# Merge operands asked for inside the last pair of sequences, and new places for the tiles around it

## The chip, the cores and the metric

The kernel runs on one core of one Trainium2 chip. A core has five engines with a queue of its own each: TensorE (PE, matrix products), VectorE (DVE), ScalarE (ACT), GpSimd (POOL) and SyncE (SP), which here issues most transfers. Each engine takes its instructions in order. The metric is the device time of one execution in microseconds (us).

## What is computed

One layer of a decoder, for a prompt of 1024 tokens and for 8 sample sequences of 4 new tokens each with 2048 old ones in a paged cache. Two mixers (a sparse attention and a short convolution) share one projection; what they give is merged, projected and followed by an MLP. Cut to the parts that the change is about:

```python
def compress(k, pe, w1, w2):            # summaries of overlapping blocks of cached rows
    chunks = ...                        # (sequence, 128 chunks of 16 rows, head, 1024)
    w1r = w1.reshape(2, 16 * 64, 256)
    proj = einsum('bckx,mxh->mbckh', chunks, w1r)
    hid = pe.reshape(-1) @ w1
    for m in range(2):
        hid = hid + proj[m, :, m:m + n_cmp]
    return gelu(hid) @ w2

def merge_and_mlp(x, a, c, ga, gb, w_nsa_out, w_conv_out, w_o, g_mlp, w_up, w_down):
    m = sigmoid(ga) * (a @ w_nsa_out) + sigmoid(gb) * (c @ w_conv_out)
    x = x + m @ w_o
    h = rms_norm(x, g_mlp)
    return x + square(relu(h @ w_up)) @ w_down
```

Every 32-bit operand of a large product is split into a high part (cast to a rounded type, fp32r) and a low part (what is left), and a product is three products: high by high, low by high, high by low.

## The kernel before

Pools of tiles are opened and closed by name on two sides of the on-chip memory, left and right, in the manner of two stacks; a tile with a tag shares `bufs` buffers with the other tiles of that tag, and a new one waits until the old one was last read. The code is written stage after stage, and a scheduler then sets the order on each engine from the dependencies and a timeline of its own; nobody writes the order by hand.

The stages around the change, in the order of the code:

1. Single units. For the first six sequences, `sample_unit` (L639) gathers one sequence's cached keys (`gth`, 1 MB), copies them by heads (`gpr`), transposes them (`ct`), splits them (`cth` on ACT, `ctl` on DVE) and multiplies them by the weight `w1` (`hid`). `blocks_out` (L484) then does the gelu: square on ACT, two operations on POOL (`gt`), tanh on ACT, a last step on DVE (`gx`), and the small products `kvc`, copied into `kcT` (keys) or `vcN` (values). These units run beside the prompt's attention.
2. Pairs. Five times (keys of 6 and 7, then values of 0 to 7) `pair_unit` (L643) does two sequences at once, with one weight product fewer: the sum of the two halves of `w1` (`w2h`, `w2l`) times the odd chunks (n = 0), and each half times a difference of chunks (`dx`, n = 1 and 2). The transposed chunks of a pair are four tiles `xt`, of six buffers; `dx` has one buffer. After n = 0 of a pair the block output of the pair before it is written (`finish()`).
3. Beside the pairs a generator `probs` does the attention of the sample tokens (`sample_group`): window rows, selected rows gathered by POOL (`gk`, four buffers of 0.5 MB), the weights through DRAM (`sl_d`), and in the end the weighted sums `so`, one column block `ownT` per group of four sequences.
4. Merge. `load_aT` (L1301) brings the prompt's attention output back from DRAM in eight tiles `at` and splits it into `aTh`, `aTl`; `load_merge` brings the rows `ta` and `cg` of a column of 128 (528 KB each), `load_wn` the column's weight (`wrd`, 256 KB; high part `whd` on ACT, low part `wld` on POOL through `wsplit`). `merge_in` (L1351) multiplies (`na`, 4 x 3 products for each of the banks 0 to 383, 384 to 767 and 768 to 1055), then DVE and POOL add `ta` and `cg`. The last bank holds the sample columns, for which the new rows of the sample attention (`ts`, from `ownT`) must be there. MJ columns do their first two banks ahead of that.
5. `wo_rows` multiplies the merge by `w_o` in two halves of columns (`wo`, then `c`); in the second half it loads the first half's rows and the input row into `x2` (L1441) and adds (L1455). Then come the norm, the transposes `xT` and the MLP.

What sets the order around the change: SP's queue, where a load waits for the buffer that it writes and everything behind it waits too; POOL's queue, which holds the gathers and the gelu operations; and the scheduler's timeline.

Of the kernel before, what the change touches and what calls it, by code (L numbers as in the profile page):

```python
# [11 lines left out]
F32 = mybir.dt.float32  # L12
F32R = mybir.dt.float32r
# [28 lines left out]
SWB = 2  # L42
MJ = 2
W1B = 9
ATTEND = 5
# [3 lines left out]
UGP = 1  # L49
EB = 3  # L50
ATT = dict(lg=3, pt=2, pv=1, gx=1, gy=1)
PB = 12
WOB = 8
QB = 12
# [65 lines left out]
def tile_hybrid_step(ctx, tc, xp, xs, cck, ccv, csk, csv, swk, swv, sconv, ptab, g_attn, w_in,  # L120
# [33 lines left out]
    def f32(ap):  # L154
        return ap.bitcast(F32)
# [280 lines left out]

    mp = open_pool("cmp", "left")
    pkh = mp.tile([128, HK, 64], F32R, name="pkh")
    pkl = mp.tile([128, HK, 64], F32R, name="pkl")
# [22 lines left out]
    def load_w1(w1, bufs, parts=True, sums=False):  # L462

        out = {}
        for lp in range(8):
            raw = w1p.tile([128, 2, 256], F32, name="w1r", tag="w1r", bufs=2)
            DMA.dma_start(raw, w1[0].rearrange("(m l p) c -> l p m c", m=2, p=128)[lp])
            if parts:
                h, l = (w1p.tile([128, 2, 256], F32R, name="w1" + x, tag="w1" + x, bufs=bufs) for x in "hl")
                S.copy(h, raw)  # L470
                V.tensor_sub(l, raw, f32(h))
                for m in range(2):
                    out[m * 8 + lp] = (h[:, m], l[:, m])
            if sums:
                h, l = (u2.tile([128, 256], F32R, name="w2" + x, tag="w2" + x, bufs=8) for x in "hl")
                V.tensor_add(raw[:, 0], raw[:, 0], raw[:, 1])
                S.copy(h, raw[:, 0])
                V.tensor_sub(l, raw[:, 0], f32(h))
                out[16 + lp] = (h, l)
        return out  # L480
# [147 lines left out]
    def by_heads(raw, q):  # L628
        by_head = up.tile([128, 2, 256], F32, name="gpr", tag="gpr")
# [12 lines left out]
    def pair_unit(kv, cache, b0, w1):  # L642
# [5 lines left out]
        for q in range(4):  # L648
            xt = u2.tile([128, 2, 512], F32, name="xt", tag="xt", bufs=6)
            for s_ in range(2):  # L650
                part = by_heads(raws[s_], q)
                pt = ps(HT["ct"], "ct")
                pv = pt.rearrange("p (i c h) -> p i c h", i=2, h=2)
                for i in range(2):
                    for h in range(2):
                        PE.transpose(pv[:, i, :, h], part[:, h, i * 128:i * 128 + 128], ident)
                S.copy(xt[:, :, s_ * 256:s_ * 256 + 256], pt.rearrange("p (i c) -> p i c", i=2))
            xs.append(xt.rearrange("p i (j e h) -> p i j e h", e=2, h=2))
# [4 lines left out]
        for n in range(3):  # L663
# [3 lines left out]
            for q in range(4):  # L667
                odd = xs[q][:, :, :nj, 1]
                if n:
                    d = up.tile([128, 2, 256], F32, name="dx", tag="gx", bufs=UG)  # L670
                    odd_, d = odd, d.rearrange("p i (j h) -> p i j h", h=2)[:, :, :nj]
                    V.tensor_sub(d, xs[q][:, :, n - 1:n - 1 + nj, 0], odd_)
                    odd = d
# [40 lines left out]

    kc = open_pool("kc", "left")
    kcT = kc.tile([128, NB, 127], F32, name="kcT")
    vcN = kc.tile([127, NB, 128], F32, name="vcN")
    chp = open_pool("cTh", "left")
# [591 lines left out]
    advance(100)  # L1310
    next(behind[0][0])
    close("pa", "cTh")
    u2 = open_pool("u2", "right")
    s1 = open_pool("s1", "left", bufs=2)
    HT.update(ct="ct", hid="hid", sk="sk", sx="sx")
    open_psum(**SMP)
    w1.update(load_w1(w1k, W1B, parts=False, sums=True))
    for i in range(ATTEND + 1, 2 * NB, 2):
# [4 lines left out]
        for n in range(3):  # L1323
            next(unit)
            if n == 0:
                finish()
            for _ in range(SSTEP[i + n % 2] * 2 // 3):
                next(probs, None)
        behind.append((unit, (kv, i % NB + 1)))
    finish()  # L1330
    close("u2", "unit", "gt", "w1")
    ap_ = open_pool("aT", "right")
    aTh = ap_.tile([128, 4, T], F32R, name="aTh")
    aTl = ap_.tile([128, 4, T], F32R, name="aTl")
    ep = open_pool("E", "right")
    wp = open_pool("w", "right", bufs=2)
# [20 lines left out]
    for j in range(MJ):  # L1357
        for i in range(2):
            merge_in(j, *BANKS[i], ("ct", "hid")[i])
    close("s1", "kc")  # L1360
    mpool = open_pool("m", "left")
# [3 lines left out]
    wop = open_pool("wo", "left", bufs=WOB)  # L1365
    for j in range(8):
# [25 lines left out]
    for i, z in enumerate(mT[2]):  # L1392
        P.tensor_copy(m9[:, :, i * 32:i * 32 + 32], f32(z[:, :, 256:]))
    close("w", "E", "aT")

    h2p = open_pool("h2", "right")
# [3 lines left out]
    fp = open_pool("F", "right", bufs=2)  # L1403
    g2 = fp.tile([128, D], F32, name="g2", bufs=1)
# [30 lines left out]
    def wo_rows(half, tt):  # L1435
# [42 lines left out]
    close("wo", "m", "cmp", "att")  # L1478


    wp = open_pool("w", "left", bufs=2)
    qp = open_pool("q", "left")

# [37 lines left out]

    hbp = open_pool("hB", "left")
    t2 = hbp.tile([128, 4, HC], F32, name="t2", tag="t2", bufs=1)
# [84 lines left out]

    rp = open_pool("T", "right")
    dp = open_pool("wd", "right")  # L1610
    wp = open_pool("w", "left")
    up = open_pool("ud", "left")
    lp = open_pool("mlp", "left")
    accp = open_pool("acc", "left")
    accs = [accp.tile([128, 4, HC], F32, name=f"acc{i}") for i in range(4)]
# [82 lines left out]

    op = open_pool("out", "right", bufs=2)
    gf = op.tile([128, D], F32, name="gf", bufs=1)  # L1700
# [126 lines left out]
```

## Time and profile before

| what | us |
|---|---|
| median of 3 timed runs | 1976.39 (1974.79 to 1979.4) |
| the profiled execution, its own time | 1969.69 |
| its span in the trace | 1967.9 |
| PE busy | 1896.1 (96%) |
| DVE, ACT, POOL busy | 1128.0, 860.5, 460.3 |

The pairs lie between about 860 and 1094 us of the span, the merge between 1110 and 1176, the two halves of `w_o` behind it up to about 1276, then the MLP to the end. A row of the trace's timeline gives the start, the duration, the engine, the line, and in brackets how long the engine had been idle and what ended that.

### The profile page before, as it was taken

Reading aid. Unit: us, or ns where it says so; the run is one execution under the profiler, and the core shown is the slowest. Engines: PE = TensorE matmul, PEld = TensorE weight load, DVE = VectorE, ACT = ScalarE, POOL = GpSimd, SP = SyncE. Lnnn points to the kernel's source line nnn. Section 1 sums busy time; section 2 is a strip of 40 time slices with the busy share of each in tenths; the row PEclk is TensorE's granted clock in tenths of the full one; section 3 lists DMA queues with packets and bytes.
Section 4 is the critical chain, followed back from the end, with each engine's and each line's share of the span. In section 5 each row is a group of like instructions: output and inputs, shape, how many; then the busy total and the mean of one; then the engine's idle time right before and its main releaser. Section 6 shows DMA issues by size and latency. Waiting matters only on the chain.

```text
span 1967.9 us, 34867 instructions
## 1 busy us (share of the span) xinstructions
PE 1896.1 (96%) x13172; PEld 1762.2 (90%) x13172; DVE 1128.0 (57%) x2367; ACT 860.5 (44%) x1905; POOL 460.3 (23%) x634
## 2 busy tenths in 40 slices
PE   9999999999999999998999699999999999999998
PEld 7999999999998888876788587789999999999998
DVE  5324232545446766657864552498676655767765
ACT  5113223555456565544542320365455444543443
POOL 3112223433444444433333250130000000000000
PEclk9999999999999999989999799999999999999999
DMA  6365316222236421176544453347756656765664
GB/s 209 126 162 136 97 55 172 65 73 65 69 90 212 148 100 50 47 230 200 180 134 143 163 180 126 122 118 246 245 189 230 225 188 240 258 185 164 182 199 157
DMA packets 238424, 303.77 MB, mean 154 GB/s; under 512 B 20725, under 2 KB 165254, under 8 KB 234160
## 3 DMA queue, kind: packets, MB, share of 16 engines
q1 hardware_dynamic: 231344, 267.99, 43.5%
q0 software_dynamic: 6912, 33.56, 5.0%
q8 instruction: 104, 1.70, 0.4%
q14 instruction: 64, 0.52, 0.1%
HBM read 222.78 MB, written 78.71 MB: 153 GB/s over the span
## 4 chain that ended last, share of the span: by engine, by line
PE 79%; DMA 9%; DVE 4%; issue 3%; ACT 3%; POOL 2%; SPq 1%; POOLq 0%; DVEq 0%; ACTq 0%
PE c L212 9%; PE c L213 9%; PE c L214 9%; PE PT L941 3%; PE ga L213 3%; PE ga L212 3%; PE ga L214 3%; PE hid L213 2%; PE hid L212 2%; DMA wrd<-sd_d 2%; PE hid L214 2%; PE pv L948 2%; PE pv L947 2%; PE so L1233 1%; PE qkv L214 1%
## 5 line engine op out<-in xcount | busy, mean ns | idle before, releaser
L212 PE MATMUL c<-ud,whd 128*128 128x264 f32 x768 | 217.8, 286 | 5.6 <-ACT whd L1623 4.3
L213 PE MATMUL c<-ud,whd 128*128 128x264 f32 x768 | 217.5, 285 | 0.0
L214 PE MATMUL c<-ud,whd 128*128 128x264 f32 x768 | 217.4, 285 | 0.0
L867 POOL TENSOR_SCALAR P<-P,st,gates 128x256 f32<-128x256 f32 (+4 forms) x272 | 151.4, 578 | 125.7 <-DVE st L863 103.7
L212 PEld LDWEIGHTS c<-ud,whd 128*128 128x128 f32 x768 | 144.5, 189 | 6.1 <-ACT whd L1623 4.5
L212 PE MATMUL c<-hBt,wuh 128*128 128x264 f32 x512 | 146.5, 286 | 2.1 <-ACT p L1512 2.1
L214 PE MATMUL c<-hBt,wul 128*128 128x264 f32 x512 | 146.1, 285 | 0.0
L213 PEld LDWEIGHTS c<-ud,whd 128*128 128x128 f32 x768 | 145.1, 189 | 0.0
L214 PEld LDWEIGHTS c<-ud,whd 128*128 128x128 f32 x768 | 144.4, 189 | 0.0
L945 DVE TENSOR_TENSOR ptl<-PT,pth 128x512 fp32r<-128x512 f32 (+1 forms) x148 | 99.4, 685 | 64.7 <-ACT pth L944 64.3
L1733 POOL MEMSET ss<- 128x1 f32 x9 | 0.8, 99 | 560.3 <-DVE ur L1655 560.3
L1623 ACT CAST whd<-wrd 128x512 fp32r<-128x512 f32 x112 | 68.2, 620 | 145.0 <-issue 97.4
L235 POOL TENSOR_TENSOR wlu<-wru,whu 128x1024 fp32r<-128x1024 f32 x32 | 76.8, 2399 | 220.8 <-ACT whu L234 220.8
L212 PE MATMUL ga<-hTh,whu 128*128 128x384 f32 (+1 forms) x384 | 127.7, 332 | 0.0
L213 PE MATMUL ga<-hTl,whu 128*128 128x384 f32 (+1 forms) x384 | 126.3, 329 | 0.0
L214 PE MATMUL ga<-hTh,wlu 128*128 128x384 f32 (+1 forms) x384 | 125.9, 328 | 0.0
L1624 DVE TENSOR_TENSOR whd<-wrd,whd 128x512 fp32r<-128x512 f32 x112 | 76.4, 690 | 77.4 <-ACT whd L1623 77.3
L944 ACT CAST pth<-PT 128x512 fp32r<-128x512 f32 (+1 forms) x148 | 83.8, 588 | 66.0 <-PE PT L941 62.7
L213 PE MATMUL c<-h2r,wuh 128*128 128x264 f32 x384 | 109.6, 285 | 1.1 <-POOL h2r L1538 0.8
L213 PE MATMUL hid<-ctl,w1h 128*128 128x254 f32 (+1 forms) x352 | 105.2, 299 | 1.7 <-DVE ctl L678 1.7
L212 PE MATMUL hid<-cth,w1h 128*128 128x254 f32 (+1 forms) x352 | 105.0, 298 | 1.7 <-ACT cth L554 1.4
L941 PE MATMUL PT<-cst,P 128*128 128x128 f32 (+1 forms) x592 | 101.0, 274 | 0.3 <-DVE st L922 0.2
(536 smaller groups left out, 6036.5 us busy)
## 6 DMA issues: line engine op xcount, KB each, us to landing
ur<-u_d SPq DMA_DIRECT2D x96, 264.0 KB
wru<-in_w_up SPq DMA_DIRECT2D x36, 512.0 KB
u_d<-u SPq DMA_DIRECT2D x64, 264.0 KB
wru<-in_w_in SPq DMA_DIRECT2D x32, 512.0 KB
h2r<-in_w_down SPq DMA_DIRECT2D x32, 512.0 KB
sd_d<-h2r SPq DMA_DIRECT2D x16, 1024.0 KB
wrd<-sd_d SPq DMA_DIRECT2D x64, 256.0 KB
wrd<-in_w_down SPq DMA_DIRECT2D x48, 256.0 KB
```

What stands on the lines that cost most here:

```text
L212: PE.matmul(out, wh, ah, start=first, stop=False)
L213: PE.matmul(out, wh, al, start=False, stop=False)
L214: PE.matmul(out, wl, ah, start=False, stop=last)
L235: (leng or P.tensor_sub)(l, raw, f32(h))
L867: P.tensor_scalar(p, p, self.st[:, br, 3, g:g + 1], gates[:, self.qi, 3 * hg + br:3 * hg + br + 1], op0=OP.mult, op1=OP.mult)
L941: PE.transpose(pt[:n, g * 128:(g + 1) * 128], pg[g], ident)
L944: S.copy(hi[:n], pt[:n])
L945: V.tensor_sub(lo[:n], pt[:n], f32(hi[:n]))
L947: PE.matmul(self.o, w, hi[:n], start=first and i == 0, stop=False)
L948: PE.matmul(self.o, w, lo[:n], start=False, stop=last and i == len(tiles) - 1)
L1623: S.copy(h, raw)
L1624: lows.append(V.tensor_sub(l, raw, f32(h)))
```

## The change

- **Loads of the merge.** At the last pair (i = 14) the pool of the weight sums is closed after n = 0 and the pools `aT` and `w` are opened. n = 0 and n = 1 each load a quarter of `aT` (256 columns now) and a merge weight, n = 2 the other two quarters; the raw data land in `xt` buffers (`room()`). The weight's low part is made on DVE instead of POOL. MJ goes from 2 to 3; the third weight is loaded behind the `ta` and `cg` rows of three columns.
- **Tiles of the pairs.** `dx` has two buffers, apart from `gx`; the `gt` of the second sequence takes the place of `mid`. `xt` goes from 6 buffers to 5, the `w1` parts from 9 to 8. `load_w1` makes the sums ahead of the parts, in a tile `both` that shares the buffers of `dx`, and leaves the raw tile as it is.
- **Close of the single units.** `finish()` runs, and the pool `unit` is closed, ahead of the first pair.
- **Behind the merge.** `wo` parts 8 to 9 buffers, `x2` 3 to 4. `kcT` and `vcN` move into the pool `cmp`. Many pools change sides.

The diff, without the pools that only change sides:

```diff
-MJ = 2
-W1B = 9
+MJ = 3
+W1B = 8
+XTB = 5
-WOB = 8
+WOB = 9
@@ load_w1
+            if sums:
+                h, l = (w2p.tile([128, 256], F32R, name="w2" + x, tag="w2" + x, bufs=8) for x in "hl")
+                both = u2.tile([128, 2, 256], F32, name="both", tag="dx", bufs=2)[:, 0]
+                V.tensor_add(both, raw[:, 0], raw[:, 1])
+                S.copy(h, both)
+                V.tensor_sub(l, both, f32(h))
+                out[16 + lp] = (h, l)
             if parts:
...
-            if sums:
-                h, l = (u2.tile([128, 256], F32R, name="w2" + x, tag="w2" + x, bufs=8) for x in "hl")
-                V.tensor_add(raw[:, 0], raw[:, 0], raw[:, 1])
-                S.copy(h, raw[:, 0])
-                V.tensor_sub(l, raw[:, 0], f32(h))
-                out[16 + lp] = (h, l)
@@ pair_unit
-            xt = u2.tile([128, 2, 512], F32, name="xt", tag="xt", bufs=6)
+            xt = u2.tile([128, 2, 512], F32, name="xt", tag="xt", bufs=XTB)
...
-                    d = up.tile([128, 2, 256], F32, name="dx", tag="gx", bufs=UG)
+                    d = u2.tile([128, 2, 256], F32, name="dx", tag="dx", bufs=2)
...
-            t = up.tile([128, 2, 256], F32, name="gt", tag="gt", bufs=UG)
+            t = u2.tile([128, 2, 256], F32, name="gt", tag=("gt", "mid")[s_], bufs=1)
@@ loads of the merge
-    def load_wn(j):
-        return wsplit(wp, w_nsa[0, :, j * 128:(j + 1) * 128], 4, 128, "d", MJ, raws=1)
+    def load_wn(j, raw=None):
+
+        if raw is None:
+            raw = ep.tile([128, 4, 128], F32, name="wnr", tag="wnr", bufs=1)
+        DMA.dma_start(raw, w_nsa[0, :, j * 128:(j + 1) * 128].rearrange("(k p) c -> p k c", p=128))
+        pool, n = (wp, 2) if j % 3 < 2 else (ep, 1)
+        h, l = (pool.tile([128, 4, 128], F32R, name="wn" + x, tag="wn" + x, bufs=n) for x in "hl")
+        S.copy(h, raw)
+        V.tensor_sub(l, raw, f32(h))
+        return h, l
+
+    def room():
+        return u2.tile([128, 2, 512], F32, name="xt", tag="xt", bufs=XTB)
 
     def load_aT(qi):
-        s = slice(qi * 128, qi * 128 + 128)
-        at = ap_.tile([128, 4, 128], F32, name="at", tag="at", bufs=2)
+        s = slice(qi * 256, qi * 256 + 256)
+        at = room().rearrange("p i (k t) -> p (i k) t", k=2)
         DMA.dma_start(at, aT_d[:, s].rearrange("(k p) t -> p k t", p=128))
-        S.copy(aTh[:, :, s], at)
-        V.tensor_sub(aTl[:, :, s], at, f32(aTh[:, :, s]))
+        for k in range(0, 4, 2):
+            S.copy(aTh[:, k:k + 2, s], at[:, k:k + 2])
+            V.tensor_sub(aTl[:, k:k + 2, s], at[:, k:k + 2], f32(aTh[:, k:k + 2, s]))
@@ units and pairs
-    next(behind[0][0])
-    close("pa", "cTh")
+    finish()
+    close("unit", "pa", "cTh")
...
+            if i == 2 * NB - 2:
+                if n == 0:
+                    close("w2")
+                    ap_ = open_pool("aT", "left")
...
+                if n < 2:
+                    load_aT(n)
+                    wns.append(load_wn(n, room()[:, 0].rearrange("p (k c) -> p k c", k=4)))
+                else:
+                    for qi in (2, 3):
+                        load_aT(qi)
...
-    for qi in range(8):
-        load_aT(qi)
     merge = [load_merge(j) for j in range(MJ)]
-    wns = [load_wn(j) for j in range(MJ)]
+    wns.append(load_wn(2))
@@ wo_rows
-            xf = fp.tile([128, D], F32, name="x2", tag="x2", bufs=3)
+            xf = fp.tile([128, D], F32, name="x2", tag="x2", bufs=4)
```

How the change moves instructions, at three places. First PE at the end of the last pair. `hid` is the pair's last product, `kvc` and `so` end the sample attention, `na` is the merge. Before:

```order
L214 MATMUL hid<-cth,w1l 128x254
L515 MATMUL kvc<-w2v,gx_11853 127x64 x4
L1246 MATMUL so<-vcN,skt 32x128
L1247 MATMUL so<-skt 32x128
L515 MATMUL kvc<-w2v,gx_11853 127x64 x4
L1246 MATMUL so<-vcN,skt 32x128
L1247 MATMUL so<-skt 32x128
L1255 MATMUL ownT<-cst,own 128x128
L212 MATMUL na<-aTh,whd 128x384
```

After:

```order
L1256 MATMUL ownT<-cst,own 128x128
L213 MATMUL na<-aTh,wnh 128x384
L214 MATMUL na<-aTl,wnh 128x384
L215 MATMUL na<-aTh,wnl 128x384
...
L1234 MATMUL so<-gk,skt 32x128 x8
...
L1234 MATMUL so<-gk,skt 32x128 x16
L519 MATMUL kvc<-w2v,gx_11870 127x64 x4
L1234 MATMUL so<-gk,skt 32x128 x8
L1247 MATMUL so<-vcN,skt 32x128
```

The `ownT` that opens these rows is that of the first group; ahead of it stands the pair's last `hid`. The first 24 `na` stand ahead of the last unit's `kvc`, and 64 `so` that stood inside the last pair stand behind its last `hid`.

Second SP's queue at the same place. Before:

```order
L1240 DMA skt<-out 4x4x128
L1241 DMA skt<-out 4x4x128
L1303 DMA at<-aT_d 128x4x128 x6
L1294 DMA ta<-ta_d 128x1056
L1294 DMA cg<-cg_d 128x1056
L1294 DMA ta<-ta_d 128x1056
L1303 DMA at<-aT_d 128x4x128 x2
L1294 DMA cg<-cg_d 128x1056
L231 DMA wrd<-in_w_nsa_out 128x4x128
```

After:

```order
L1302 DMA xt<-in_w_nsa_out 128x4x128
L1315 DMA xt<-aT_d 128x4x256
L1302 DMA xt<-in_w_nsa_out 128x4x128
L1224 DMA skt<-sl_d 128x512 x2
L1315 DMA xt<-aT_d 128x4x256 x2
L1224 DMA skt<-sl_d 128x512
L1224 DMA skt<-sl_d 128x256
L1241 DMA skt<-out 4x4x128
L1242 DMA skt<-out 4x4x128
L1295 DMA ta<-ta_d 128x1056
...
L1302 DMA wnr<-in_w_nsa_out 128x4x128
```

`aT` and two weights moved ahead of the last loads of the sample attention (`skt`); the six loads of `ta` and `cg` are left behind them, and the third weight (`wnr`) behind those.

Third PE at the first pair. Before:

```order
L214 MATMUL hid<-cth,w1l 128x254
L509 MATMUL kvc<-gx,w2k 64x127 x4
L656 MATMUL ct<-cst,gpr 128x128 x8
L1102 MATMUL skT<-cst,swn 128x128 x8
L1135 MATMUL sn<-kcT,qbd 32x127
```

After:

```order
L215 MATMUL hid<-cth,w1l 128x254
L513 MATMUL kvc<-gx,w2k 64x127 x8
L660 MATMUL ct<-cst,gpr 128x128 x8
L1136 MATMUL sn<-kcT,qbd 32x127
L1137 MATMUL sn<-newT,qbd 32x4
```

The `kvc` of the last single unit, which stood 62 rows further down inside the first pair, now stand ahead of the pair's first transposes `ct`.

## Rows read from the trace of the kernel before

**Rows 1.** The page, part 1: busy us, share of the span, instructions of each engine.

```profile
PE 1896.1 (96%) x13172; PEld 1762.2 (90%) x13172; DVE 1128.0 (57%) x2367; ACT 860.5 (44%) x1905; POOL 460.3 (23%) x634
```

**Rows 2.** Stretches: length, busy PE, PEld, DVE, ACT, POOL, clock, DMA share, GB/s.

```profile
1010.00:1020.00 10.00, 6.81 (x48) 6.60 (x48) 5.67 (x9) 2.85 (x5) 2.37 (x2) 0.87 0.87 332
1080.00:1090.00 10.00, 10.00 (x87) 8.41 (x87) 3.55 (x6) 1.34 (x3) 0.00 (x0) 1.00 0.01 2
1094.00:1110.00 16.00, 6.95 (x30) 4.77 (x29) 8.66 (x16) 6.13 (x11) 4.37 (x4) 0.56 0.53 166
1110.00:1176.00 66.00, 53.99 (x292) 51.56 (x293) 34.64 (x57) 21.06 (x40) 32.60 (x29) 0.87 0.63 208
1110.00:1120.00 10.00, 4.57 (x14) 4.07 (x15) 3.08 (x8) 3.34 (x6) 1.27 (x1) 0.51 0.93 327
...
1270.00:1280.00 10.00, 6.76 (x37) 5.08 (x36) 3.21 (x7) 4.70 (x13) 1.49 (x4) 1.00 0.74 200
```

**Rows 3.** Waits of PE, 1094 to 1176: us in total, times, longest us.

```profile
PE na L212 <- ACT whd L234: 10.4, 4, 5.2
PE kvc L515 <- DVE gx L492: 5.2, 1, 5.2
PE so L1246 <- DVE vcN L522: 2.9, 2, 1.8
PE na L214 <- POOL wld L235: 1.4, 4, 0.7
PE ownT L1255 <- DVE own L1253: 1.2, 1, 1.2
```

**Rows 4.** Timeline of PE, end of the pairs to the first `wo`.

```profile
1082.95 1.53 PE L1233 MATMUL so<-gk,skt 128*32 128x128 f32 x16
...
1094.30 0.28 PE L213 MATMUL hid<-ctl,w1h 128*128 128x254 f32 x1
1094.41 0.28 PE L214 MATMUL hid<-cth,w1l 128*128 128x254 f32 x1
...
1115.90 0.69 PE L212 MATMUL na<-aTh,whd 128*128 128x384 f32 x1 [5.18 <-ACT whd L234]
1116.39 0.53 PE L213 MATMUL na<-aTl,whd 128*128 128x384 f32 x1
1116.71 0.53 PE L212 MATMUL na<-aTh,whd 128*128 128x384 f32 x1
...
1121.49 0.34 PE L212 MATMUL na<-aTh,whd 128*128 128x384 f32 x1
1121.67 0.34 PE L213 MATMUL na<-aTl,whd 128*128 128x384 f32 x1
...
1175.40 0.39 PE L212 MATMUL wo<-woh,mT0h 128*128 128x512 f32 x1
```

**Rows 5.** SP's queue over the merge loads.

```profile
1091.13 12.64 SPq L1303 DMA_DIRECT2D at<-aT_d  x6
...
1108.57 0.64 SPq L231 DMA_DIRECT2D wrd<-in_w_nsa_out  x1
```

**Rows 6.** Tile `gk` in 1000 to 1100: issue to landing of its gathers.

```profile
DMA to landing us min/median/max: 4.1/4.4/6.7
```

**Rows 7.** Timeline of PE and of DVE at the first pair.

```profile
860.16 1.79 PE L656 MATMUL ct<-cst,gpr 128*128 128x128 f32 x8 [3.24 <-DVE kcT L511]
...
858.59 0.43 DVE L476 TENSOR_TENSOR w1r<-w1r 128x256 f32<-128x256 f32 x1 [2.78 <-DMA w1r<-in_cmp_w_k]
```

**Rows 8.** Timeline of DVE and of PE in the pairs.

```profile
1015.78 0.43 DVE L635 COPY gpr<-gth 128x512 f32<-128x512 f32 x1 [4.33 <-DMA gth<-in_cache_cmp_v,idx]
...
1090.21 0.69 DVE L678 TENSOR_TENSOR ctl<-dx,cth 128x508 fp32r<-128x508 f32 x1 [0.76 <-ACT cth L677]
...
1092.39 0.69 DVE L678 TENSOR_TENSOR ctl<-dx,cth 128x508 fp32r<-128x508 f32 x1 [0.76 <-ACT cth L677]
...
1017.45 0.58 PE L213 MATMUL hid<-ctl,w2h 128*128 128x256 f32 x1 [3.19 <-DVE ctl L678]
```

**Rows 9.** Timeline of DVE and of PE in the second half of `w_o`.

```profile
1271.88 0.69 DVE L1455 TENSOR_TENSOR x<-c,x 128x512 f32<-128x512 f32 x1 [3.09 <-DMA x<-in_x_prompt]
...
1277.36 0.99 PE L1419 MATMUL xT<-cst,xn 32*128 32x32 f32 x8 [1.81 <-DVE hA0l L1426]
```

**Rows 10.** Timeline of DVE and of POOL beside each other in the merge.

```profile
1127.37 1.31 DVE L1386 TENSOR_TENSOR wol<-wor,woh 128x512 fp32r<-128x512 f32 x1
...
1126.86 1.26 POOL L1355 TENSOR_TENSOR ta<-ta,cg 128x384 f32<-128x384 f32 x1 [0.96 <-DVE ta L1354]
```

More of the change, by code (lines that the diff above doesn't have):

```diff
@@ L437, in tile_hybrid_step @@
     mp = open_pool("cmp", "left")
+    kcT = mp.tile([128, NB, 127], F32, name="kcT")
+    vcN = mp.tile([127, NB, 128], F32, name="vcN")
     pkh = mp.tile([128, HK, 64], F32R, name="pkh")
@@ L628, in by_heads @@
     def by_heads(raw, q):
-        by_head = up.tile([128, 2, 256], F32, name="gpr", tag="gpr")
+        by_head = up.tile([128, 2, 256], F32, name="gpr", tag="gpr", bufs=2)
         src = raw[:, q * 512:(q + 1) * 512].rearrange("c (l h d) -> c l h d", h=2, d=64)
@@ L712, in finish @@
             have.add(key)
-    kc = open_pool("kc", "left")
-    kcT = kc.tile([128, NB, 127], F32, name="kcT")
-    vcN = kc.tile([127, NB, 128], F32, name="vcN")
     chp = open_pool("cTh", "left")
@@ L1310, in tile_hybrid_step @@
     advance(100)
-    next(behind[0][0])
-    close("pa", "cTh")
-    u2 = open_pool("u2", "right")
-    s1 = open_pool("s1", "left", bufs=2)
+    finish()
+    close("unit", "pa", "cTh")
+    s1 = open_pool("s1", "right", bufs=2)
+    up = u2 = open_pool("u2", "right")
+    w2p = open_pool("w2", "right")
     HT.update(ct="ct", hid="hid", sk="sk", sx="sx")
@@ L1328, in tile_hybrid_step @@
                 next(probs, None)
+            if i == 2 * NB - 2:
+                if n == 0:
+                    close("w2")
+                    ap_ = open_pool("aT", "left")
+                    aTh = ap_.tile([128, 4, T], F32R, name="aTh")
+                    aTl = ap_.tile([128, 4, T], F32R, name="aTl")
+                    wp = open_pool("w", "left")
+                    wns = []
+                if n < 2:
[4 more added lines that the diff above has]
+                        load_aT(qi)
         behind.append((unit, (kv, i % NB + 1)))
     finish()
[L1331 to L1336, printed above, removed]
-    for qi in range(8):
-        load_aT(qi)
+    close("u2")
+    ep = open_pool("E", "left")
     merge = [load_merge(j) for j in range(MJ)]
-    wns = [load_wn(j) for j in range(MJ)]
+    wns.append(load_wn(2))
     for _ in probs:
@@ L1359, in tile_hybrid_step @@
             merge_in(j, *BANKS[i], ("ct", "hid")[i])
-    close("s1", "kc")
-    mpool = open_pool("m", "left")
+    close("s1", "gt", "w1")
+    mpool = open_pool("m", "right")
     mT = [[mpool.tile([128, KT, c1 - c0], F32R, name=f"mT{c0}{x}") for x in "hl"] for c0, c1 in BANKS]
     open_psum(**GEMM)
-    wop = open_pool("wo", "left", bufs=WOB)
+    wop = open_pool("wo", "right", bufs=WOB)
     for j in range(8):
@@ L1393, in tile_hybrid_step @@
         P.tensor_copy(m9[:, :, i * 32:i * 32 + 32], f32(z[:, :, 256:]))
-    close("w", "E", "aT")
-    h2p = open_pool("h2", "right")
+    close("E", "w", "aT", "cmp", "att")
+    h2p = open_pool("h2", "left")
     hA = [[h2p.tile([128, 4, HC], F32R, name=f"hA{q}{x}") for x in "hl"] for q in range(2)]
@@ L1402, in tile_hybrid_step @@
     (r11, r12), (r21, r22) = h2r
-    fp = open_pool("F", "right", bufs=2)
+    fp = open_pool("F", "left", bufs=2)
     g2 = fp.tile([128, D], F32, name="g2", bufs=1)
@@ L1477, in tile_hybrid_step @@
             transpose_h2(*behind_wo.pop(0))
-    close("wo", "m", "cmp", "att")
-    wp = open_pool("w", "left", bufs=2)
-    qp = open_pool("q", "left")
+    close("wo", "m")
+    wp = open_pool("w", "right", bufs=2)
+    qp = open_pool("q", "right")
     def part(tag, bufs=1):
@@ L1520, in tile_hybrid_step @@
     open_psum(c=4)
-    hbp = open_pool("hB", "left")
+    hbp = open_pool("hB", "right")
     t2 = hbp.tile([128, 4, HC], F32, name="t2", tag="t2", bufs=1)
@@ L1603, in tile_hybrid_step @@
     close("hB", "q", "w", "h2")
[L1609 to L1614, printed above, removed]
+    rp = open_pool("T", "left")
+    dp = open_pool("wd", "left")
+    wp = open_pool("w", "right")
+    up = open_pool("ud", "right")
+    lp = open_pool("mlp", "right")
+    accp = open_pool("acc", "right")
     accs = [accp.tile([128, 4, HC], F32, name=f"acc{i}") for i in range(4)]
@@ L1694, in tile_hybrid_step @@
     close("wd", "T")
-    op = open_pool("out", "right", bufs=2)
+    op = open_pool("out", "left", bufs=2)
     gf = op.tile([128, D], F32, name="gf", bufs=1)
```

## Prediction

> **What bounds the kernel now.** I read the page's table of engines first: TensorE (PE) is busy 1896.1 of 1967.9 us, so about 72 us of the span are all that any reordering can win, plus what is lost where PE works at half clock [rows 1]. Next the table of stretches, to find where those 72 us lie [rows 2]. The stretch 1080 to 1090, the middle of the last pair of sequences, has PE at 10.00 of 10 and the DMA engines at 0.01. Right behind it, 1094 to 1110 has PE busy 6.95 of 16 us at a granted clock of 0.56, and 1110 to 1176 has 53.99 of 66 at 0.87. That is 21 us of idle PE, and more lost to the clock. The list of PE's waits in 1094 to 1176 names what ended them: the gelu of the last unit (5.2), the copies and sums of the sample columns (2.9 and 1.2), and four times the cast of a merge weight (10.4 in all) [rows 3]. The timeline of PE and SP's queue shows why: the merge (na) starts only at 1115.90, because its operands are asked for when the pairs are over, the aT tiles from 1091.13, the weight at 1108.57 [rows 4, 5]. The engines that move data were idle while PE was full, and full (0.93, 327 GB/s) while PE was idle [rows 2].
>
> How much of it is excess: the merge is 8 columns of 36 products. At full clock they stand 0.18 us apart for 384 columns (1121.49, 1121.67) and in proportion 0.133 for 288, so 8 x 12 x (0.176 + 0.176 + 0.133) = 46.6 us. The last unit's kvc, so and ownT are some 2.5 us of work at full clock. From the start of that stretch (1094.4) to the first wo product (1175.40) are 81.0 us [rows 4]. Excess: 81.0 - 46.6 - 2.5 = about 32 us.
>
> **Part 1, merge operands loaded in the last pair, three columns ahead.** By the order on PE 24 products of the merge, with eight so among them, now follow the last hid directly, and 48 stand before the second group's ownT; before, all stood behind it. 64 so products moved from inside the last pair to behind it: no new work, 64 x 0.09 us (16 in 1.53 us at 1082.95 [rows 4]), but they no longer fill holes there. What I expect to remain of the 32 us:
>
> First columns: the second half of aT is cast on ScalarE and VectorE just ahead of the last unit's own vector work, where a low part of this size takes 0.69 us [rows 8]; 0 to 3, I take 1.5. The gelu chain, 5.2 us of idle PE before [rows 3], has 24 merge products (4.2 us) and 16 so products over it; I take 1. If that cover went, the 5.2 would be back.
>
> Third column: its weight is the one load that stays behind the six rows of ta and cg on SP's queue. These are 6 x 0.54 = 3.24 MB; at 327 GB/s [rows 2] 9.9 us, the weight's 0.26 MB another 0.8, landing and cast and low part some 3: 13.7 us. Beside it PE has about 10 us: 24 products at 0.176, the third banks of two columns 24 x 0.133, so and ownT. So some 4 us of idle, and each such hole also costs clock: behind the 5.2-us wait products stand 0.32 apart (1116.39, 1116.71) rather than 0.18 for about 4 us [rows 4], which is 2 us lost. I take 6, with 0 and 10 as ends.
>
> The nearest row for a queued load is the first weight, asked at 1108.57 and used by PE at 1115.90, 7.3 us for 0.26 MB behind other traffic [rows 4, 5]. The Trainium skill, "DMA: Bandwidth & Descriptors", section "Anatomy of one DMA", gives about 2.0 us plus bytes over 436 GB/s for a transfer from GpSimd's queue; taken as an estimate for these 3.5 MB it would be 10 us, the third column would hardly wait, and the sum below would be about 5 us better. The trace has moved no more than 327 GB/s in that stretch, and gathers of 0.52 MB landed after 4.4 us at the median where the page would have 3.2 [rows 2, 6]; I stay with the rows.
>
> Later columns (weights of 3 to 7, behind cg and ta): the waits for casts other than the first, 10.4 - 5.2 = 5.2, of which 3.0 belonged to the third column, and 1.4 for low parts [rows 3]; I keep 3.5. Remaining: 1.5 + 1 + 6 + 3.5 = 12.
>
> The last pair pays too. Its last so groups need gathers of 0.52 MB in four buffers, and these now share the DMA engines with 2.1 MB of aT and 0.5 MB of weights; all of this is some 10 MB in about 32 us, 320 GB/s, close to the 327 above. GpSimd's gelu operations for the last unit are queued behind ten of these gathers, each of which waits for a so group. I take 2 us (0 to 8). The casts of aT stand in VectorE's queue ahead of the pair's own differences: 1.5 (0 to 3). Gain of part 1: 32 - 12 - 3.5 = 16.5 us, ends 8 and 24.
>
> Moving the weights' low parts from GpSimd to VectorE: a low part takes GpSimd's queue out of the path (1.4 us of PE's waits [rows 3]) and puts 0.69 on VectorE. A VectorE low part that ran beside GpSimd's ta addition took 1.31, the addition 1.26 [rows 10]. The Trainium skill, "SBUF — State Buffer", section "SBUF: two separate sides", says that a VectorE operation with two SBUF inputs and a GpSimd operation that reads SBUF exclude each other; the rows agree, and by it six columns could lose 6 x 0.6 = 3.7 us. VectorE is busy 34.64 of 66 us there [rows 2], so without that rule or with it I charge nothing.
>
> **Part 2, units closed before the pairs.** The last single unit's block output used to run inside the first pair. Now both its kvc and the one before stand ahead of the pair's first ct on PE. Before, PE waited 3.24 us there (860.16), because VectorE stood at a w1 sum that waited for its DMA (858.59) [rows 7]. Now it waits for a gelu chain, and the nearest row for that is the 5.2 of the last unit [rows 3]: 2 us more. Ends 0 (the sums' DMA no longer in the way earlier) and 4.
>
> **Part 3, difference tiles, five xt, eight w1 tiles.** With one dx tile a difference, its cast and its low part take turns: starts of low parts are 2.2 us apart (1090.21, 1092.39) for 12 products of 1.4 us (0.12 apart, 1094.30 and 1094.41) [rows 4, 8]. Two tiles let the next difference run under the cast; most of the time the so products hide this, as PE is full in 1080 to 1090 [rows 2]. On the other side, five xt tiles leave the next pair one place instead of two ahead of the old pair's last product, so the gathers' buffers come free one step, some 2 us, later. One gather already shows: VectorE waited 4.33 us for it at 1015.78 and PE 3.19 at 1017.45, at a clock of 0.87 over those 10 us [rows 2, 8], so 3.2 + 1.3 = 4.5. Ends: -6 (stall and small waits gone) and +8 (two more such); I take +1.
>
> **Part 4, fourth x2 tile.** VectorE waited 3.09 us at 1271.88 for a row of the second wo half that was asked for too late, and PE is idle 3.24 of 1270 to 1280 [rows 2, 9]. With four tiles that load is asked one row block earlier. What is late next is the 1.81 for a low part of h at 1277.36 [rows 9]. I take -3 (0 to -5).
>
> The sides of the pools, the renamed weights and the rest of the order (the MLP stands as before) I cost at nothing: no engine gets work there that it didn't have.
>
> **Sum.** -16.5 + 2 + 1 - 3 = -16.5 us. The profiled run is 1969.69, so 1953.2 there; the median of the timed runs is 1976.39, 6.7 above it, so I forecast 1960 for the median.
>
> **Rivals.** (a) Half the gain: the last pair's gathers and the aT loads crowd each other (8 instead of 2) and the third weight costs 10 instead of 6, so the gain is about 16.5 - 10 and with the rest 6.5: 1968 to 1970. For it speaks the 0.93 of 1110 to 1120, against it the 0.01 of 1080 to 1090 [rows 2]. (b) More: the third weight hides and the pairs' stalls go with the second dx tile (6 + 6 on top): 1948. (c) The change doesn't do what it says: aT or the first weights land so late in the last pair that na starts no earlier; the gain of part 1 is nought and 2 + 1 - 3 = 0 is left: 1976. Against it, the DMA engines had nothing to do in 1080 to 1090 [rows 2]. (d) Slower: the pair boundaries. If each of the four boundaries between pairs has its gather exposed, 3.2 + 2 for the later release and 2 of clock, 7 us each, 28 in all less the 4.5 that is there: +23.5 in place of +1, 1976.4 - 17.5 + 23.5 = 1982. It eats the whole gain from 5.5 us a boundary on. For it, the one stall of the trace is of this kind; against it, it is the only one of that length in 860 to 1094, and the order keeps some 35 to 50 products between a gather and its use, as before (35 to 65).
>
> **Chances.** Forecast 0.50 (1952 to 1967 for itself), (a) 0.17, (b) 0.10, (c) 0.11, (d) 0.12. A measurement of this kernel can tell about 0.2%, 4 us, from no change. Faster: 0.50 + 0.17 + 0.10 = 0.77; same 0.11; slower 0.12. The range goes from below (b) to (c): 1945 to 1976; it leaves out (d) and half of (c).
>
> **What would show it.** Right: na products within 1 us of the last hid, PE's waits between last hid and first wo at 10 to 14 us instead of 21, one of them 3 to 6 us for the cast of the third weight, the granted clock near 1.0 in the first 10 us behind the last hid, no wait for x2 in the second wo half, and 5 us of wait at the first pair's ct. Wrong: PE waiting for a gather or for kvc in the last pair, waits for gth at several boundaries, or na held up by aTl.

## The result

The changed kernel takes 1961.04 us in the median of 4 runs (1955.19 to 1965.28), the kernel before 1976.57 (4 runs); the ratio is 0.9918, 95% interval 0.9889 to 0.9947. The forecast was 1960, the range 1945 to 1976. Five more runs, beside new ones of the kernel before, gave 1960.02 against 1974.52, 0.9928 (0.9914 to 0.9941). The time is the forecast one; the sum by which I came to it is not, as the traces and the experiments show. So the agreement is in part luck.

First the changed kernel's waits of PE, from the list over the whole span (the columns are us in total, times, longest us), then its stretches behind the last pair (columns as in [rows 2]):

```profile
PE na L213 <- ACT wnh L1305: 10.9, 3, 4.1
PE kvc L513 <- DVE gx L496: 5.3, 1, 5.3
...
PE so L1234 <- DMA skt<-sl_d: 3.7, 1, 3.7
PE skT L1103 <- DMA swn<-in_state_win_k: 3.1, 1, 3.1
```

```profile
1086.90:1110.00 23.10, 23.10 (x169) 19.51 (x169) 6.06 (x13) 3.57 (x7) 7.49 (x8) 1.00 0.69 250
1110.00:1169.80 59.80, 48.18 (x271) 46.16 (x270) 36.86 (x67) 19.45 (x38) 23.86 (x23) 0.91 0.47 159
```

The first stretch is what the change was to do: where PE was busy 6.95 of 16 us at a clock of 0.56 [rows 2], it is busy 23.10 of 23.10 at 1.00. The merge starts 0.15 us behind the last hid, where it took 21.5 us [rows 4], and the last unit's kvc and so no longer wait for the gelu chain. But the 10.4 us of waiting for a weight's cast [rows 3] are not less: they are 10.9, three waits in place of four, all in the second stretch. And the 5.2 for a gelu chain [rows 3] has an answer of 5.3 at another place: it is the kvc ahead of the first pair (L513, keys). The 3.7 for skt is new.

The timeline of PE at these places:

```profile
863.03 1.12 PE L513 MATMUL kvc<-gx,w2k 128*64 128x127 f32 x8 [5.29 <-DVE gx L496]
...
1050.17 1.54 PE L1234 MATMUL so<-gk,skt 128*32 128x128 f32 x8 [3.67 <-DMA skt<-sl_d]
...
1086.83 0.28 PE L215 MATMUL hid<-cth,w1l 128*128 128x254 f32 x1
...
1086.98 0.42 PE L213 MATMUL na<-aTh,wnh 128*128 128x384 f32 x1
...
1118.41 0.44 PE L213 MATMUL na<-aTh,wnh 128*128 128x384 f32 x1 [3.59 <-ACT wnh L1305]
...
1132.47 0.69 PE L213 MATMUL na<-aTh,wnh 128*128 128x384 f32 x1 [3.21 <-ACT wnh L1305]
...
1149.98 0.69 PE L213 MATMUL na<-aTh,wnh 128*128 128x384 f32 x1 [4.07 <-ACT wnh L1305]
```

To set the stages against each other I took, from the timelines of two executions each, the starts of the named products (us; the second trace of each kernel is from the first two experiments below):

| from ... to | before | before, again | changed | changed, again |
|---|---|---|---|---|
| last hid of the single units to first ct of the pairs | 4.1 | 4.9 | 7.7 | 7.6 |
| to the last hid of the pairs | 234.3 | 235.3 | 222.3 | 219.9 |
| to the last wo of the first half | 128.2 | 128.3 | 129.9 | 129.1 |
| to the last xT | 71.9 | 71.7 | 72.8 | 73.0 |
| to the last product | 666.2 | 669.4 | 666.2 | 665.4 |

The second and the third line have to be read together, since so products moved from the pairs into the stretch behind. By the traces 64 stand there, but 4 of them stood there before; 56 of the 60 that moved are those of gathered rows (line L1234, two records each), and these last 12.95 us together (busy PE and PEld of L1234 alone, then clock, DMA share, GB/s):

```profile
1086.90:1216.90 130.00, 12.95 (x112) 11.33 (x112) 0.96 0.51 172
```

With these moved back in thought, the pairs by themselves are as long as before (234.1 us on average, 234.8 before), and the stretch behind is 11.8 us shorter. With 3.2 us more ahead of the pairs and 1.1 more in the second half of w_o the traces give about 8 us, 10 to 11 with the ends; the medians give 14.5 to 15.5. Single executions of the changed kernel lie up to 10 us apart, those of the kernel before up to 15, so a difference of less than about 4 us between two pairs of traces says little.

### The profile page after: what moved, and what is told of

Same layout as the page of the kernel before. It is cut to its first block, busy times and chain, and to the rows that moved or that the text cites. A ratio compares the mean times of both kernels' runs of the same rounds, so it can differ in the third digit from the quotient of the medians.

```text
span 1963.5 us, 34847 instructions
## 1 busy us (share of the span) xinstructions
PE 1898.9 (97%) x13172; PEld 1766.6 (90%) x13172; DVE 1129.9 (58%) x2375; ACT 859.0 (44%) x1905; POOL 443.8 (23%) x626
## 4 chain that ended last, share of the span: by engine, by line
PE 70%; DMA 5%; DVE 4%; ACT 2%; POOL 1%; issue 1%; SPq 0%; DVEq 0%; POOLq 0%; ACTq 0%
PE c L213 9%; PE c L214 9%; PE c L215 9%; PE PT L942 3%; PE ga L214 3%; PE ga L213 3%; PE ga L215 3%; PE hid L214 2%; PE hid L215 2%; PE hid L213 2%; DMA wrd<-sd_d 2%; PE pv L949 2%; PE pv L948 2%; PE so L1234 1%; PE sl L1195 1%; PE skT L1103 1%
## 5 line engine op out<-in xcount | busy, mean ns | idle before, releaser
L215 PE MATMUL hid<-cth,w1l 128*128 128x254 f32 (+1 forms) x352 | 99.7, 283 | 0.0
```

The source lines that it names most:

```text
L215: PE.matmul(out, wl, ah, start=False, stop=last)
```

## The experiments

**Both kernels once more**, unedited.

> The changed kernel once more, unchanged, for a second trace and more timed runs. Two executions of it differed by 10 us so far, and the one trace is 4.4 us shorter than that of before where the medians differ by 15.5. If the medians tell the truth, five more rounds give a ratio of 0.990 to 0.994. If the traces do, 0.996 to 0.999. The waits that the first trace shows behind the last pair (3.6, 3.2 and 4.1 us for casts of merge weights) should be there again within 1 us, since the order of the instructions sets them; those for gathers and loads in the pairs (3.1 for swn, 3.7 for skt) may come and go.

> The kernel before once more, unchanged, for a second trace of it. Its first trace was 6.7 us under the median of its timed runs. I expect 1972 to 1980, a ratio of 0.998 to 1.002, and a trace in which the stretch from the last hid to the first wo of the second half is again 128 us within 2, while the pairs (860 to 1094 in the first trace) are longer, by up to 7 us: that is where a late gather can cost.

The changed kernel: 1960.02 (5 runs), 0.9928. The medians tell the truth; the one trace of it was a long execution, and the one of before a short one (the second spans 1973.5, the first 1967.9). The waits for casts came back at 3.59, 2.50 and 3.98 us, that for skt too (3.47), and that for swn as 2.6 us in two waits. The kernel before gave 0.9979 (0.9964 to 0.9993) against itself, so a ratio is good to about 0.2%, not better.

**The loads put back behind the pairs.** The pools aT and w are opened behind `close("u2")`, the loads in the last pair go, and the raw data land in a pool that takes u2's place:

```diff
     finish()
     close("u2")
+    rwp = open_pool("raw", "right")
...
+    def room():
+        return rwp.tile([128, 2, 512], F32, name="rw", tag="rw", bufs=4)
+
+    for qi in range(4):
+        load_aT(qi)
+    for j in range(2):
+        wns.append(load_wn(j, room()[:, 0].rearrange("p (k c) -> p k c", k=4)))
```

> The changed kernel, but aT and the first two merge weights are loaded into a pool of their own that takes the place of the pairs' tiles, so that they start only when the pairs are over; all else stays (three columns ahead, two dx tiles, five xt, four x2 tiles). Theory 1: the gain is that of the loads in the last pair, 9 to 17 us; this kernel then is within 4 us of before, 1970 to 1978. Theory 2: the gain comes from the tiles of the pairs and the closed unit, and the loads bring little; then it stays at 1958 to 1964. The so products should move back into the last pair, and PE should stand 5 us before the first na.

1964.98, 0.9954 (0.9941 to 0.9968). Neither theory: the early loads are worth 5 us (0.9954 less 0.9928, with some 4 us of uncertainty), and 9 us of the gain stay without them. Which other part of the change gives these 9 us no run shows by itself. PE's waits behind the last hid (columns as above), and two stretches, the pairs and the rest up to the last wo:

```profile
PE na L213 <- ACT wnh L1305: 18.5, 4, 12.7
PE ownT L1256 <- DVE own L1254: 1.2, 1, 1.2
PE kvc L519 <- DVE gx L496: 1.0, 1, 1.0
...
860.70:1077.80 217.10, 212.86 (x1553) 168.56 (x1553) 152.30 (x289) 100.43 (x189) 74.82 (x77) 0.99 0.56 180
1077.80:1211.50 133.70, 111.30 (x594) 97.66 (x594) 55.17 (x97) 29.96 (x56) 31.35 (x31) 0.91 0.53 175
```

The merge has its wait back, 12.7 us and not the 5 that I expected. But about half of the moved so products still stands behind the last hid, so the gelu chain costs 1.0 us and not 5.2, and in the pairs PE is idle 217.1 - 212.9 = 4.2 us. The same stretch of the changed kernel and of the one before, second traces:

```profile
862.00:1082.10 220.10, 211.79 (x1506) 167.76 (x1506) 155.90 (x293) 104.54 (x196) 72.19 (x75) 0.96 0.57 184
...
861.80:1097.30 235.50, 223.67 (x1633) 176.44 (x1633) 156.20 (x299) 102.97 (x195) 76.54 (x72) 0.98 0.52 166
```

8.3 us idle in the changed kernel, 11.8 before. Without the early loads the pairs have 7.6 us less of idle PE than before; with them 3.5 less, at a lower clock (0.96 against 0.99). The wait for skt is 3.5 us with the loads and 1.3 without. The waits for swn (2.6 in the changed kernel's second trace, none worth naming here) come ahead of the first of the loads and are no effect of them. The so products behind the last hid (L1234 alone, as above) last 6.80 us here:

```profile
1077.60:1211.50 133.90, 6.80 (x65) 6.23 (x64) 0.91 0.53 175
```

With them counted back the pairs take 224 us (216.8 from the first ct to the last hid, and 6.8) and the stretch behind 127 (133.7 less 6.8). In the changed kernel it is 234 and 116.5. So in the traces the early loads win some 10 us behind the pairs and lose some 10 in them; what is left of this, the 5 us, is read from the medians alone.

**The third weight ahead of ta and cg.**

```diff
+    wns.append(load_wn(2))
     merge = [load_merge(j) for j in range(MJ)]
-    wns.append(load_wn(2))
```

> The changed kernel, but the third merge weight is loaded ahead of the six rows of ta and cg instead of behind them. In the changed kernel's trace PE waits 3.6 us for its cast. Theory 1: the load is late because 3.24 MB are ahead of it on SP's queue; then the wait goes and 3 to 5 us with its half clock, 1955 to 1958. Theory 2: the load had landed and ScalarE's queue was held by the first mT casts, which wait for the sample tiles' memory until ownT is done; then too the wait goes, since the cast now stands ahead of them, but the later weights (3.2 and 4.1 us) wait as before or longer, and the time falls by 0 to 3 us.

1951.04, 0.9868 (0.9852 to 0.9883), 9 to 12 us under the changed kernel, more than either theory gave. From the last hid to the last wo it is 119.7 us instead of 129.1 and 129.9. None of the three waits is left:

```profile
PE na L214 <- DVE aTl L1370: 2.2, 1, 2.2
PE na L213 <- ACT aTh L1369: 1.6, 1, 1.6
PE na L215 <- DVE wnl L1306: 0.8, 1, 0.8
```

On the cause theory 2 was right. In the changed kernel's trace the third weight is asked for at 1100.94 and cast at 1117.76 (first two rows of SP's queue, the first of the six loads ahead of it and the weight's own), and ScalarE's timeline tells what it did in between:

```profile
1096.57 0.35 SPq L1295 DMA_DIRECT2D ta<-ta_d  x1
...
1100.94 0.50 SPq L1302 DMA_DIRECT2D wnr<-in_w_nsa_out  x1
...
1095.80 0.63 ACT L495 ACTIVATE gt<-gt 128x508 f32<-128x508 f32 x1 [0.59 <-POOL gt L494]
1114.90 0.52 ACT L1397 ACTIVATE mT0h<-ta 128x384 fp32r<-128x384 f32 x1 [18.48 <-PE ownT L1256]
1115.34 0.51 ACT L1397 ACTIVATE mT384h<-ta 128x384 fp32r<-128x384 f32 x1
...
1117.33 0.52 ACT L1397 ACTIVATE mT384h<-ta 128x384 fp32r<-128x384 f32 x1 [0.74 <-POOL ta L1377]
1117.76 0.60 ACT L1305 CAST wnh<-wnr 128x512 fp32r<-128x512 f32 x1
```

It stood 18.48 us at the first mT cast, whose tile takes the memory of the sample attention's pool and so waits for the last ownT. The weight's cast was queued behind it. The transfers had ended before: the semaphore records of the trace have the weight landed at 1111.15, and the row of DMA throughput in 40 slices of 1096 to 1120 us (0.6 us each, GB/s) falls to nothing at 1112, with the weight and two tiles of w_o behind it all landed.

```profile
GB/s 0 24 115 141 324 411 412 386 377 371 393 368 416 433 428 414 408 422 437 394 388 371 330 366 233 123 34 0 0 0 0 0 0 0 0 0 0 0 0 0
```

What both theories missed is that the raw tile of the later weights has one buffer. The third weight held it until its low part was done at 1119.4, so the fourth was asked for at 1119.41, the next again late, and the one lateness ran through the columns. With the load first the cast is at 1100.38:

```profile
1100.38 0.62 ACT L1305 CAST wnh<-wnr 128x512 fp32r<-128x512 f32 x1 [4.32 <-DMA wnr<-in_w_nsa_out]
1118.06 0.52 ACT L1397 ACTIVATE mT0h<-ta 128x384 fp32r<-128x384 f32 x1 [17.07 <-PE ownT L1256]
```

The mT cast waits as long as before, and nothing suffers from it.

**One difference tile in the changed kernel.**

```diff
-                both = u2.tile([128, 2, 256], F32, name="both", tag="dx", bufs=2)[:, 0]
+                both = u2.tile([128, 2, 256], F32, name="both", tag="dx", bufs=1)[:, 0]
...
-                    d = u2.tile([128, 2, 256], F32, name="dx", tag="dx", bufs=2)
+                    d = u2.tile([128, 2, 256], F32, name="dx", tag="dx", bufs=1)
```

> The changed kernel with one buffer for the differences instead of two (for the sums of w1 too); the order of the sample attention changes with it: all but two of the so groups' products stand inside the pairs again. Theory 1: two tiles are what makes the pairs shorter (unit's last hid to last hid 227 to 230 in the changed kernel with 64 so moved out of it, 238 to 240 before); with one, PE waits at cth and ctl again and the kernel is 4 to 10 us slower than the changed one, 1964 to 1970. Theory 2: the second tile buys nothing, because so products fill the same holes, and it even moves the sample attention 20 to 30 us later, with its wait for skt of 3.5 us; then one tile gives 1952 to 1960.

1984.27, 1.0048 (1.0029 to 1.0068): slower than the kernel before, and 24 us slower than the changed kernel. Theory 1 has the sign and less than half of the size. From the units' last hid to the last wo it takes 375.7 us, where the changed kernel takes 356.7 and 359.9. The waits that the trace names in the pairs are small (third row: hid for ctl 5.4 in three waits):

```profile
PE na L213 <- ACT wnh L1305: 8.8, 3, 4.5
PE kvc L513 <- DVE gx L496: 5.7, 1, 5.7
PE hid L214 <- DVE ctl L682: 5.4, 3, 2.9
```

ScalarE shows the shared tile: in the pairs its casts wait 37.9 us for the differences, where the changed kernel has 6.9 (first and second row, in the stretches from the first ct to the last hid). PE is idle there 247.7 - 232.8 = 14.9 us (third row, columns as in [rows 2]), and 8.3 in the changed kernel's second trace.

```profile
ACT cth L681 <- DVE dx L676: 37.9, 17, 7.0
...
ACT cth L681 <- DVE dx L676: 6.9, 7, 2.2
...
862.94:1110.60 247.66, 232.79 (x1637) 177.66 (x1637) 161.46 (x300) 106.66 (x199) 72.91 (x78) 0.98 0.54 173
```

So the tile costs PE something in the pairs. But the order differs in more than the tile: the so products are back in the pairs and no longer cover the end. How the 24 us divide between the two, this run doesn't tell.

**One difference tile and the third weight early.**

> One difference tile and the third merge weight ahead of ta and cg, both against the changed kernel. If the two act apart from each other, the time is that of the kernel with one tile less the 9 us that the early third weight gave: 1943 to 1951 by theory 2 of the tiles, 1955 to 1961 by theory 1.

1971.89, 0.9987 (0.9973 to 1.0001). Both ranges are missed, since one tile costs more than either theory had. But it is 12 us under the run with one tile alone: the early third weight brings there what it brings with two tiles. The two act apart from each other.

**The pairs' tiles in the kernel before**, first both edits, then the five xt tiles alone:

```diff
-            xt = u2.tile([128, 2, 512], F32, name="xt", tag="xt", bufs=6)
+            xt = u2.tile([128, 2, 512], F32, name="xt", tag="xt", bufs=5)
...
-                    d = up.tile([128, 2, 256], F32, name="dx", tag="gx", bufs=UG)
+                    d = u2.tile([128, 2, 256], F32, name="dx", tag="dx", bufs=2)
```

> The kernel before with one edit to the pairs' tiles: two buffers for the differences, apart from gx, and five xt tiles instead of six (the same memory). Nothing else of the change. The changed kernel with one difference tile was 24 us slower than with two, and the changed kernel with its loads behind the pairs kept 9.5 of the 15.5 us. Theory 1: the second difference tile shortens the pairs by itself, 6 to 12 us against before: 1963 to 1969. Theory 2: the 24 us are the price of one tile in the changed kernel alone (where the sums of w1 share it, and its order is another); then this edit gives 1973 to 1978.

> The kernel before with five xt tiles instead of six and nothing else. Theory 1: a place less for the next pair lets gathers come late, and this alone costs 5 to 12 us (1980 to 1987), which the two difference tiles pay for in the changed kernel. Theory 2: the sixth tile is of no use: 1973 to 1977, the same as before.

1970.1, 0.999 (0.9978 to 1.0001), and 1972.19, 1.0000 (0.9987 to 1.0013). The sixth xt tile was of no use. The second difference tile is worth about 2 us in the kernel before, 4 at the most by the interval; the first time lies between the two theories' ranges, nearer to the second. So most of the 24 us is a price of the changed kernel. There the sums of w1 take turns with the differences in that tile; that this is the reason isn't shown.

**Three x2 tiles in the changed kernel.**

```diff
-            xf = fp.tile([128, D], F32, name="x2", tag="x2", bufs=4)
+            xf = fp.tile([128, D], F32, name="x2", tag="x2", bufs=3)
```

> The changed kernel with three x2 tiles as before. Theory 1: the fourth tile is worth 1 to 3 us (PE idle 3.2 us before there, 1.7 after): 1961 to 1964, and the wait of VectorE for x2 and PE's 1.8 and 1.4 us are back. Theory 2: it is worth nothing, since from the first wo to the last transposes the two kernels differ by 1 us the wrong way: 1959 to 1961.

1961.2, 0.9924 (0.9908 to 0.994): the same as with four. VectorE's wait for the load is there again (2.29 us, from the first row), and in the changed kernel's own trace (second row) VectorE waits at the same place for PE instead:

```profile
1266.41 0.69 DVE L1477 TENSOR_TENSOR x<-c,x 128x512 f32<-128x512 f32 x1 [2.29 <-DMA x<-in_x_prompt]
...
1271.51 0.69 DVE L1477 TENSOR_TENSOR x<-c,x 128x512 f32<-128x512 f32 x1 [1.49 <-PE c L215]
```

**Weights ahead of aT in the last pair, and two raw tiles.** Both stand on the kernel with the early third weight, the second on the first:

```diff
                 if n < 2:
-                    load_aT(n)
                     wns.append(load_wn(n, room()[:, 0].rearrange("p (k c) -> p k c", k=4)))
+                    load_aT(n)
```

```diff
-            raw = ep.tile([128, 4, 128], F32, name="wnr", tag="wnr", bufs=1)
+            raw = ep.tile([128, 4, 128], F32, name="wnr", tag="wnr", bufs=2)
```

> The third weight ahead of ta and cg, and in the last pair each merge weight (256 KB) is loaded ahead of its quarter of aT (512 KB), against the changed kernel. Only 256 KB then stand on SP's queue ahead of the sample weights skt, for which PE waits 2.5 to 3.7 us. Theory 1: that wait is the aT load's doing; it falls to 1 to 2 us, and with the clock behind it the time is 2 to 4 us under that with the third weight alone (1951): 1947 to 1949. Theory 2: the wait is the round trip of the weights through DRAM, and it stays: 1950 to 1952.

> The changed kernel with the third weight ahead of ta and cg, the merge weights ahead of aT in the last pair (1947.4 so far), and two raw tiles for the later merge weights instead of one. In the trace without the second raw tile PE waits once more, 3.2 us, for a weight's cast. Theory 1: that weight was asked for late because its one raw tile was taken: the wait goes, 1942 to 1946. Theory 2: it is ScalarE's queue, where the cast stands behind casts of the w_o weights that wait for their loads: it stays, 1946 to 1949.

1947.36, 0.9865 (0.9844 to 0.9885): the same as without the swap (0.9868), and the wait for skt is 2.5 us in both traces (3.5 to 3.7 in those of the changed kernel, 1.3 where no load stands ahead). So a load ahead of skt seems to cost 1 to 2 us there, and whether it is of 256 or 512 KB can't be seen. With two raw tiles 1942.61, 0.9846 (0.9827 to 0.9866): the intervals overlap, but the wait of 3.2 us for a later weight's cast, which the run with the swap had, is gone, as theory 1 said.

**The pairs' PSUM banks opened ahead of the last unit's output**, on top of these:

```diff
-    finish()
-    close("unit", "pa", "cTh")
+    next(behind[0][0])
+    HT.update(ct="ct", hid="hid", sk="sk", sx="sx")
+    open_psum(**SMP)
+    finish()
+    close("unit", "pa", "cTh")
...
-    HT.update(ct="ct", hid="hid", sk="sk", sx="sx")
-    open_psum(**SMP)
```

> The kernel with the third weight early, weights ahead of aT and two raw tiles, and besides the PSUM banks of the pairs are opened ahead of the last single unit's block output, so that sample scores (sn) stand under its gelu chain. PE waits 5.2 to 5.5 us for that chain in every run with the units closed early. Theory 1: the wait falls to 2 to 4 us and the time by 2 to 4. Theory 2: the transposes of the first pair still stand behind kvc, since their tiles take the unit's memory; the time stays within 2 us of the run without this edit.

1941.4, 0.9834 (0.9821 to 0.9847). The wait falls by 1 us only (first row: the longest wait in the run; second: the same in the run without this edit), and the time is not told apart from that run: theory 2. In the trace the sample scores do stand under the gelu chain now, and the transposes of the first pair still behind kvc (864.35 and 865.40).

```profile
PE kvc L513 <- DVE gx L496: 4.3, 1, 4.3
...
PE kvc L513 <- DVE gx L496: 5.3, 1, 5.3
```

This kernel and the one with two raw tiles are the best of all: 30 and 31 us under the kernel before, and by the ratios 16 and 19 under the changed one.

## Why the prediction was right, and where it was not

The time was right. Four of its terms were mis-sized or had the wrong cause, and their errors cancel in part; this is luck.

- *First columns and the covered chain (1.5 + 1 left).* Right: PE is full for 23 us behind the last hid, at full clock.
- *Third column (6 us left), later columns (3.5 left).* Here the step failed. The wait of 3.6 us at the third column is near the 4 that I worked out, but from a wrong cause: not 3.24 MB on SP's queue but ScalarE's queue, held by a tile whose memory was not free. The overlap was wrong too: from the first of these loads (1096.57) to the last ownT (1114.5) PE had some 18 us of work and not about 10, since so products and kvc stand there as well. The loads were not faster than I took them for: the weight landed 14.6 us after that first load was asked for, and up to 1112.2, when the traffic ended, the mean is 327 GB/s again (the row below). With 18 us of work beside them the third column would not have waited for the loads. The Trainium skill, "DMA: Bandwidth & Descriptors", section "Anatomy of one DMA", gives about 2.0 us plus bytes over 436 GB/s for a transfer from GpSimd's queue; the estimate of 10 us that the prediction had from this is further from the 14.6 us than its sum from the rows. What I missed besides is that the lateness runs on: 3.2 and 4.1 us at later columns. The early third weight shows the price of all of it, some 10 us; it is near the 9.5 that I had left for both, by another cause, and it could be had back.

```profile
1096.57:1112.20 15.63, 15.63 (x112) 12.64 (x111) 2.48 (x6) 0.00 (x0) 3.52 (x4) 1.00 0.88 327
```

- *The last pair (3.5).* Also a failed step in its detail. What the loads met there was not the gathers but the sample weights skt on their way through DRAM, 3.5 to 3.7 us, and then a clock of 0.66 (the row below). By the trace of the run with the late loads the price of the loads in the pairs is some 10 us and not 3.5. The so products that moved I had counted as 64 (60 by the trace) and sized at 0.09 us each, from 16 in 1.53 us; but the trace holds two records for each of them (256 for 128), so it was 0.19 us, and as they now stand 0.23 (12.95 us for 56).

```profile
1050.00:1060.00 10.00, 9.83 (x67) 8.96 (x69) 1.70 (x4) 0.56 (x2) 1.59 (x2) 0.66 0.08 22
```

- *Tiles of the pairs (+1, from -6 to +8).* Mis-sized: by the same trace the pairs without the early loads are some 11 us shorter than before (224 against 234.8), and which part of the change does this is not shown. In the changed kernel the price of the loads takes it away again, so that the pairs are as long as before. My rival of late gathers, to which I gave 12%, is not there: five xt tiles cost nothing, and while VectorE still waits for gathers (9.9 us in three waits in the pairs of the first trace), PE's wait of 3.19 behind one [rows 8] has no answer; none of its waits for ctl there is over 0.9.
- *Units closed early (+2).* 3.2 by the traces, by the mechanism named: 5.2 to 5.7 us for a gelu chain in each of the runs with this edit but the last.
- *Fourth x2 tile (-3).* Wrong. It is worth nothing. I read VectorE's wait [rows 9] as PE's loss; PE's own waits there are for the transposes' copies (1.40 us for h2r in each run of the changed kernel), and they stay.
- *Loads in the last pair as the main gain.* Right in sign, too large in size: 5 us by themselves, where I had 16.5 for part 1. The so products behind the last hid are another gain: they cover the gelu chain even when the loads are late (1.0 us instead of 5.2).

What stays open: the traces account for 8 to 11 us of a difference of 14.5 to 15.5 between medians, which part of the change gives the 9 us that stay without the early loads is not shown, and why one difference tile costs 24 us in the changed kernel was only narrowed down.

## What to carry to other kernels

When operands are asked for earlier, follow them to the engine that prepares them: a cast that is queued behind one whose tile is not yet free comes late, however early its data land. Look for single buffers in a chain of loads: one late use makes all that follow late. When loads are moved under other work, look for what that work loses by them, too. And before a wait of a helping engine is priced as a gain, look whether the bounding engine has a wait of its own there that ends later.

## What the runs showed of the hardware

The loads of the merge moved 397 GB/s on average in 1099 to 1110 of the changed kernel (up to 437 in 0.6 us), with gathers beside them, and 366 in 1106 to 1117 of the kernel before. The 327 of [rows 2] is no bound: its last 3 us, in which the traffic ran out, had 216 (first row changed, the others before).

```profile
1099.00:1110.00 11.00, 11.00 (x76) 8.38 (x75) 1.26 (x3) 0.00 (x0) 0.33 (x1) 1.00 1.03 397
...
1106.00:1117.00 11.00, 3.50 (x12) 2.18 (x12) 3.96 (x11) 2.71 (x5) 1.07 (x1) 0.50 1.02 366
...
1117.00:1120.00 3.00, 3.00 (x11) 2.79 (x11) 0.84 (x2) 1.24 (x2) 0.20 (x1) 0.53 0.64 216
```

Products with 32 columns of weights: 16 records last 1.94 us in the changed kernel's timeline (the row below), and 1.53 in the kernel before (1082.95 in [rows 4]). The single records in the two traces tell the difference: in a run of them they start 0.11 us apart in both, and at 1082.95 two such runs overlap.

```profile
1100.97 1.94 PE L1234 MATMUL so<-gk,skt 128*32 128x128 f32 x16
```

The low part on VectorE that took 1.31 us beside GpSimd [rows 10] has its like in the changed kernel: mT384l, beside the second of two additions on GpSimd that ended at 1117.29, took 1.34 us, and 0.55 a moment later.

```profile
1115.03 2.26 POOL L1377 TENSOR_TENSOR ta<-ta,cg 128x384 f32<-128x384 f32 x2 [3.39 <-issue]
...
1116.37 1.34 DVE L1398 SCALAR_TENSOR_TENSOR mT384l<-ta,mT384h 128x384 fp32r<-128x384 f32 x1
...
1118.24 0.55 DVE L1398 SCALAR_TENSOR_TENSOR mT384l<-ta,mT384h 128x384 fp32r<-128x384 f32 x1
```
